# A hybrid SSD / attention block on one core: rotation, scan normalization and two scan sums on VectorE instead of GpSimd, key halves by DMA, and a different preparation of down blocks

## The chip, the core and the metric

The kernel is one launch on one core of a Trainium2 chip, in float32. What is timed is the device time of the launch in microseconds (us). TensorE (PE in the profile) multiplies matrices, VectorE (DVE), ScalarE (ACT) and GpSimd (POOL) do elementwise work, SyncE (SP) issues transfers; ACT and POOL issue transfers too, and each engine works through its own instructions in order.

## The reference

One block of a network for 512 tokens of width 2048. `u @ w_in` gives all projections at once; one half of the width goes through a state space scan (SSD), the other through attention with 16 query heads over 4 key heads in three branches (compressed, selected and window keys), of which the last two work on rotated queries and keys. Both halves meet in `w_out`; a gated feed-forward layer of width 5632 follows.

```python
def partial_rope(x, cos, sin):
    half = ROPE_DIM // 2                      # ROPE_DIM = 16 of 64
    c, s = cos[None, :, None, :], sin[None, :, None, :]
    x1, x2 = x[..., :half], x[..., half:ROPE_DIM]
    return jnp.concatenate([x1 * c - x2 * s, x2 * c + x1 * s, x[..., ROPE_DIM:]], axis=-1)
# ssd_mixer ends in
    return rmsnorm(y * jax.nn.silu(z), norm_w)
# nsa_mixer
    q_rot = partial_rope(q, cos, sin)
    ks, kw = partial_rope(ks, cos, sin), partial_rope(kw, cos, sin)
    k_cmp = compress_tokens(kc, cmp_w1_k, ...)   # silu(blocks @ w1) @ w2
    ...
    o = g[..., 0, :] * o_cmp + g[..., 1, :] * o_sel + g[..., 2, :] * o_win
# the block
    u = rmsnorm(h, attn_norm_w)
    z, xbc, dt_raw, q, kc, vc, ks, vs, kw, vw, gate_raw = split(u @ w_in)
    h = h + concatenate([y_ssd, y_att]) @ w_out
    v = rmsnorm(h, ffn_norm_w)
    h = h + (silu(v @ w_gate) * (v @ w_up)) @ w_down
    return rmsnorm(h, final_norm_w)
```

## The kernel before, in words

**Products in three passes.** A float32 product is made of three matmuls of a faster type (float32r): each operand is split into a high part and the rest. `a_hi` (L127) writes the high part with ScalarE, `lo` (L130) subtracts it and writes the low part, mostly with VectorE; `mul` (L136) and `add` (L139) are the other two helpers, called with the engine that is to do the work. Since all of them have one line each in the profile, groups are told apart by their tiles: `whi`/`wlo` are the two parts of a weight piece, `w1h`/`w1l` those of the compression's weight, `uq`, `rq` and `kh`/`kl` those of unrotated queries, rotated queries and rotated keys, `pth`/`ptl` those of transposed attention weights, `R` those of an item of the feed-forward layer.

**Up to 700 us: one stream of projection matmuls with other work let in.** `run_unit` (L235) runs one unit after the other: 128 columns of `w_in` or `w_out`, in pieces of four 128x128 blocks. `issue_split` splits a piece three pieces ahead (`LEAD`), and `sch.tick()` (`Sched`, L76) after each three matmuls lets generators go on: a `yield 6` means "go on after six more ticks", and `sch.wait` waits for a flag. The generators are the evacuations of finished units (`ev_z`, `ev_kc`, `ev_vs`, `ev_ks`, `ev_q`), the key compression (`compress`, L663) and `attention` (L851). PE's order follows from these ticks; in this part the order of the other engines is made by a scheduler, which runs a model of the engines.

- `ev_z` (L587) forms y·silu(z) for eight pieces t, sends it to DRAM (`gy_d`) and adds its squares into `acc2`, by GpSimd (L615 calls `add`, the profile has L139, tile `acc`). Behind the eighth, `ms_parts` (L638) loads each piece, multiplies it by the norm's row with GpSimd (tile `gy`), and splits it with the norm's weight as a scale.
- `compress` loads 16 pieces of w1 by transfers on GpSimd's queue (L676, `w1r`, four buffers), splits them and multiplies.
- `rope` (L775) sends the two swapped 8-row halves of each of two heads to a tile `sw` by four transfers on GpSimd's queue, while VectorE multiplies by cosines (`ro`); `rope2` (L786) multiplies `sw` by signed sines and adds, both by GpSimd. `q_stack` (L816) splits queries into two halves each: for `uq` GpSimd makes the low parts, for `rq` VectorE. `ev_ks` writes each rotated key half into both partition halves: eight splits, of which GpSimd makes two low parts.
- `attention` walks 112 items (4 groups, 4 heads, 7 blocks): `score` (matmuls, mask, exponential), `norm` (L920: reciprocal of the sum, times the gate, times the weights; it follows `score` in the same step), `trans` (transposes, three steps later: `LAG`), and `pvmm`. `compressed` (L858) does the compressed branch of a group.

**From 700 us: seven products instead of eight.** Gate, up and down use Strassen's scheme: of a block's four quarters 11, 12, 21, 22 seven combinations M1 to M7 are multiplied (Winograd's variant). Here every engine's order is written out. `steps` is the list of products and `items` that of their weights. `run_step` calls `prep(i + 2)` (L1235): `form` (L1219) makes an item's remaining sum on VectorE and its high part on ScalarE, `prep` its low part on VectorE; `form(i + 1)` is called ahead of the low part of i. `advance` (L1185) starts loads in list order whenever a buffer is free. The down projection takes 35 visits (`VISITS`): column block j, n rows of blocks. `quad` (L1392) gives a visit's combinations: S1 = 21 + 22 by GpSimd from loaded blocks (M5; M6 is 11 + S1), and S3 = 21 + 11 (M7), in visits 0 to 5 by GpSimd, later by a load on SP and a second, accumulating transfer on GpSimd's queue (L1208, L1210).

## Time and profile before

| | us |
|---|---|
| the three runs | 2185.95, 2178.3, 2175.37 (median 2178.3) |
| the profiled execution | 2179.35 |
| its span (first to last instruction) | 2177.5 |
| PE busy / DVE / ACT / POOL in the span | 2138.7 / 1778.4 / 1209.2 / 438.2 |
| granted TensorE clock, mean | 0.994 |

The profile is of one execution. A group row of it names line, engine, operation, the tiles it writes and reads with their shape, the count, then the busy time and the mean of one, then how long the engine sat idle just before such instructions and on whom it waited. A timeline row has the start, the length, the instruction, and in brackets the idle time before it with the engine that ended it. A window row has, for a stretch of time, the busy time of each engine with its number of instructions, the granted clock (1 is full), the share of the transfer engines and what they moved.

### The profile page before, as it was taken

How to read it: one execution, taken by the hardware profiler on the slowest of the kernel's cores; microseconds unless marked ns; L12 is line 12 of the kernel's file. 1: busy time of each engine (PE TensorE's matmuls, PEld its weight loads, DVE VectorE, ACT ScalarE, POOL GpSimd, SP SyncE). 2: the span in 40 equal slices, each digit the busy share in tenths (PEclk: the TensorE clock that was granted, in tenths of full speed). 3: DMA queues.
4: the chain of work that ended last, by engine and by line, in shares of the span. 5: the costliest groups of instructions: out<-in, count | busy, mean ns of one | idle time of the engine just before them, and what ended most of it. 6: DMA issues, size and time to landing. Idle time of an engine off the chain costs nothing.

```text
span 2177.5 us, 35329 instructions
## 1 busy us (share of the span) xinstructions
PE 2138.7 (98%) x12832; PEld 1890.0 (87%) x12832; DVE 1778.4 (82%) x2802; ACT 1209.2 (56%) x2023; POOL 438.2 (20%) x443
## 2 busy tenths in 40 slices
PE   9999999999999999999999999999999999999997
PEld 7888887888788888888888888888888899999897
DVE  6799767878886659888888888888888878887796
ACT  6555446686676657555555555555555443443353
POOL 0002234424431134100000000000000222222232
PEclk9999999999999999999999999999999999999999
DMA  6222342223464487888888788887888879888973
GB/s 214 92 69 73 129 139 88 76 98 110 142 214 116 110 256 211 242 220 252 219 255 239 216 260 213 253 239 218 254 220 264 312 192 326 240 275 211 315 197 100
DMA packets 179582, 428.22 MB, mean 197 GB/s; under 512 B 20784, under 2 KB 27952, under 8 KB 179408
## 3 DMA queue, kind: packets, MB, share of 16 engines
q1 hardware_dynamic: 140192, 322.74, 44.2%
q0 software_dynamic: 29552, 85.87, 20.2%
q10 hardware_dynamic: 9664, 17.36, 2.2%
q8 instruction: 101, 1.65, 0.3%
q14 instruction: 73, 0.60, 0.1%
HBM read 359.83 MB, written 62.39 MB: 194 GB/s over the span
## 4 chain that ended last, share of the span: by engine, by line
PE 84%; DVE 5%; DMA 4%; ACT 2%; issue 2%; POOL 1%; SPq 0%; DVEq 0%; ACTq 0%; POOLq 0%
PE ps_s L1269 21%; PE ps_g L1269 11%; PE ps_g L254 7%; PE ps_g L252 7%; PE ps_g L253 7%; PE ps_t L1269 6%; PE ps_g L1275 2%; PE ps_g L1273 2%; PE ps_g L1274 2%; PE ps_t L1275 2%; PE ps_t L1273 2%; PE ps_s L1275 2%; PE ps_t L1274 2%; PE ps_s L1273 2%; PE ps_s L1274 2%
## 5 line engine op out<-in xcount | busy, mean ns | idle before, releaser
L127 ACT ACTIVATE R<-Z 128x1024 fp32r<-128x1024 f32 (+4 forms) x444 | 405.9, 926 | 379.7 <-DVE Z L139 284.6
L130 DVE TENSOR_TENSOR R<-Z,R 128x1024 fp32r<-128x1024 f32 (+4 forms) x352 | 374.4, 1073 | 28.2 <-ACT R L127 9.8
L252 PE MATMUL ps_g<-u,whi 128*128 128x512 f32 x778 | 318.4, 409 | 2.1 <-ACT whi L127 2.1
L254 PE MATMUL ps_g<-u,wlo 128*128 128x512 f32 x778 | 307.2, 395 | 0.2
L253 PE MATMUL ps_g<-u,whi 128*128 128x512 f32 x778 | 306.1, 393 | 0.0
L1269 PE MATMUL ps_s<-u,R 128*128 128x512 f32 (+1 forms) x1160 | 251.3, 347 | 0.1
L1269 PEld LDWEIGHTS ps_s<-u,R 128*128 128x128 f32 x1160 | 188.7, 188 | 27.4 <-ACT A L1484 0.4
L130 DVE TENSOR_TENSOR wlo<-wraw,whi 128x512 fp32r<-128x512 f32 x203 | 154.6, 765 | 57.6 <-ACT whi L127 53.1
L127 ACT ACTIVATE whi<-wraw 128x512 fp32r<-128x512 f32 x203 | 125.9, 625 | 105.4 <-PE ps_g L253 85.6
L254 PEld LDWEIGHTS ps_g<-u,wlo 128*128 128x128 f32 x778 | 146.4, 188 | 33.1 <-DVE wlo L130 1.8
L252 PEld LDWEIGHTS ps_g<-u,whi 128*128 128x128 f32 x778 | 146.9, 189 | 24.9 <-ACT whi L127 2.4
L253 PEld LDWEIGHTS ps_g<-u,whi 128*128 128x128 f32 x778 | 147.4, 189 | 22.7
L1269 PE MATMUL ps_g<-u,R 128*128 128x512 f32 (+1 forms) x600 | 131.4, 347 | 0.0
L1269 PE MATMUL ps_t<-u,R 128*128 128x512 f32 x592 | 131.2, 348 | 0.0
L1269 PE MATMUL ps_g<-T,R 128*128 128x512 f32 (+1 forms) x584 | 125.6, 346 | 0.0
L1269 PE MATMUL ps_s<-V,R 128*128 128x512 f32 (+1 forms) x568 | 123.4, 348 | 0.0
L1269 PE MATMUL ps_s<-T,R 128*128 128x512 f32 (+1 forms) x552 | 122.9, 349 | 0.2 <-DVE R L130 0.2
L130 DVE TENSOR_TENSOR E<-Z,R 128x1024 fp32r<-128x1024 f32 (+1 forms) x92 | 110.8, 1204 | 7.5 <-ACT R L127 3.5
L139 DVE TENSOR_TENSOR Z<-Z 128x1024 f32<-128x1024 f32 (+4 forms) x99 | 107.8, 1088 | 5.0 <-POOL Z L139 3.2
L1269 PEld LDWEIGHTS ps_g<-u,R 128*128 128x128 f32 x600 | 98.0, 188 | 14.0
L1269 PEld LDWEIGHTS ps_t<-u,R 128*128 128x128 f32 x592 | 96.9, 188 | 14.0
L139 DVE TENSOR_TENSOR A<-ps_g,A 128x512 f32<-128x512 f32 (+1 forms) x102 | 67.3, 664 | 50.8 <-PE ps_g L1269 38.1
(520 smaller groups left out, 5561.8 us busy)
## 6 DMA issues: line engine op xcount, KB each, us to landing
Z<-in_w_up SPq DMA_DIRECT2D x95, 512.0 KB, 4.7
Z<-in_w_gate SPq DMA_DIRECT2D x95, 512.0 KB, 5.6
wraw<-in_w_in SPq DMA_DIRECT2D x156, 256.0 KB, 2.6
g_d<-A SPq DMA_DIRECT2D x147, 256.0 KB, 6.4
Z<-in_w_gate POOLq DMA_DIRECT2D x37, 512.0 KB, 7.7
Z<-in_w_up POOLq DMA_DIRECT2D x37, 512.0 KB, 7.9
u<-g_d SPq DMA_DIRECT2D x70, 256.0 KB, 5.4
Z<-in_w_down SPq DMA_DIRECT2D x55, 320.0 KB, 4.7
```

Of the source, the lines that this page charges most:

```text
L127: act.activation(dst, src, AF.Copy, scale=scale)
L130: eng.tensor_tensor(dst, src, f(hi), ALU.subtract)
L139: eng.tensor_tensor(o, a, b, ALU.add)
L252: pe.matmul(p, hi_t[i][:, j, :], ah, start=(k == 0), stop=False)
L253: pe.matmul(p, hi_t[i][:, j, :], al, start=False, stop=False)
L254: pe.matmul(p, lo_t[i][:, j, :], ah, start=False, stop=(k == u.nk - 1))
L1269: pe.matmul(o, w, x, start=start, stop=(k == n - 1 and o is q), skip_group_check=not fresh[0])
L1273: pe.matmul(q, h[:, k, :], ah, start=(k == 0), stop=False)
L1274: pe.matmul(q, h[:, k, :], al, start=False, stop=False)
L1275: pe.matmul(q, l[:, k, :], ah, start=False, stop=(k == s.blk.n - 1))
```

## The change

1. `ev_z`: the square sums of pieces 2 and 3 are added by VectorE.
2. `ms_parts`: VectorE multiplies by the norm's row and weight in one instruction, and the split takes no scale any more.
3. `rope`: VectorE multiplies by sines (`sw`) and by cosines (`ro`), and four accumulating transfers on GpSimd's queue add the swapped halves of `sw` into `ro`. `rope2` is gone, the sines' sign in the table is turned, and two cleared tiles aren't wanted any more.
4. `ev_ks`: each key half is split once, and a transfer copies both parts to the other partitions. `ev_q`: the low parts of `uq` are made by VectorE.
5. `norm`: it runs one step later; the reciprocals of two sides are one instruction; for the first side the product with the gate is made by ScalarE. `compressed` of group 0 has 10 ticks ahead of its transposes instead of 6.
6. Down: visits 22 to 27 form S3 by GpSimd from loaded blocks, as visits 0 to 5 do. In visit 0, the low part of an item is made before the sum of the next one (`late_sum`).

```diff
--- before.py
+++ after.py
@@ -23,6 +23,7 @@
 VISITS = [(0, 5), (1, 3), (2, 5), (3, 5), (4, 5), (5, 5), (6, 4), (7, 6), (1, 4), (6, 4), (3, 5), (4, 5), (2, 5), (5, 5),
           (0, 5), (7, 5), (1, 5), (6, 5), (2, 5), (7, 5), (5, 6), (0, 6), (3, 6), (4, 6), (1, 4), (6, 4), (2, 4),
           (0, 6), (2, 3), (6, 5), (7, 6), (5, 6), (3, 6), (4, 6), (1, 6)]
+BY_POOL = list(range(6)) + list(range(22, 28))
 GRING = 7
 WARM = 10
 NRAW0 = 2 * KD // 4
@@ -612,7 +613,7 @@
             else:
                 sq = sp.tile([128, 512], F32, tag="sq" if g == 0 else "yz", name="sq", bufs=1)
                 act.activation(sq, zs, AF.Square)
-                add(pool, acc2, acc2, sq)
+                add(dve if t in (2, 3) else pool, acc2, acc2, sq)
             sch.flags.add(("gy", t))
             if t == 7:
                 yield 12
@@ -623,15 +624,11 @@
 
     P2 = {}
 
-    def parts(dst, t, scale=None):
+    def parts(dst, t):
         h = wp.tile([128, 512], F32R, tag="whi", name="hp", bufs=4)
         l = wp.tile([128, 512], F32R, tag="wlo", name="lp", bufs=4)
-        if scale is None:
-            a_hi(h, t)
-            lo(dve, l, t, h)
-        else:
-            a_hi(h, t, scale=scale)
-            dve.scalar_tensor_tensor(l, t, scale, f(h), op0=ALU.mult, op1=ALU.subtract)
+        a_hi(h, t)
+        lo(dve, l, t, h)
         nc.gpsimd.dma_start(dst[0], f(h))
         nc.gpsimd.dma_start(dst[1], f(l))
 
@@ -641,9 +638,9 @@
             yield 8
             t = wp.tile([128, 512], F32, tag="raw", name="gy", bufs=4)
             nc.sync.dma_start(t, gy_d[k])
-            mul(pool, t, t, P2["row2"])
+            dve.scalar_tensor_tensor(t, t, col(C_SN + k), P2["row2"], op0=ALU.mult, op1=ALU.mult)
             yield 2
-            parts(gp_d[k], t, col(C_SN + k))
+            parts(gp_d[k], t)
             sch.flags.add(("gp", k))
 
     def ev_kc(g):
@@ -770,23 +767,16 @@
             sch.flags.add(("v", g))
         return ev
 
-    swt = []
-
     def rope(ap, qs):
 
-        R["nsw"] = R.get("nsw", 0) + 1
-        sw = swt[R["nsw"] % 2]
-        for b in (0, 64):
-            nc.gpsimd.dma_start(sw[b:b + 8, :], qs[b + 8:b + 16, :])
-            nc.gpsimd.dma_start(sw[b + 8:b + 16, :], qs[b:b + 8, :])
+        sw = ap.tile([128, 512], F32, tag="sw", name="sw", bufs=2)
+        mul(dve, sw, qs, ropes)
         ro = ap.tile([128, 512], F32, tag="ro", name="ro", bufs=1)
         mul(dve, ro, qs, ropec)
-        return sw, ro
-
-    def rope2(ap, sw, ro):
-        t = ap.tile([128, 512], F32, tag="fo", name="ro2", bufs=1)
-        mul(pool, t, sw, ropes)
-        add(pool, ro, ro, t)
+        for b in (0, 64):
+            nc.gpsimd.dma_start(ro[b:b + 8, :], sw[b + 8:b + 16, :], accum_op=ALU.add)
+            nc.gpsimd.dma_start(ro[b + 8:b + 16, :], sw[b:b + 8, :], accum_op=ALU.add)
+        return ro
 
     def ev_ks(g):
         def ev(p):
@@ -794,22 +784,17 @@
             ap = pools["att"][1]
             t = ap.tile([128, 512], F32, tag="qs", name="kt", bufs=2)
             mul(dve, t, p, rrow)
-            sw, ro = rope(ap, t)
+            ro = rope(ap, t)
             yield 4
-            rope2(ap, sw, ro)
             yield from after(("a", g - 2))
-            kh = ap.tile([128, 2, 512], F32R, tag="kh", name="kh", bufs=2)
-            kl = ap.tile([128, 2, 512], F32R, tag="kl", name="kl", bufs=2)
+            ks = ap.tile([128, 2, 2, 512], F32R, tag="ks", name="ks", bufs=2)
             for br in range(2):
-                s = ro[br * 64:br * 64 + 64, :]
                 own = slice(br * 64, br * 64 + 64)
-                for r in range(2):
-                    d = slice(r * 64, r * 64 + 64)
-                    a_hi(kh[d, br, :], s)
-                for r in range(2):
-                    d = slice(r * 64, r * 64 + 64)
-                    lo(dve if r == br else pool, kl[d, br, :], s, kh[own, br, :])
-            R["k", g] = (kh, kl)
+                d = slice(64 - br * 64, 128 - br * 64)
+                a_hi(ks[own, br, 0, :], ro[own, :])
+                lo(dve, ks[own, br, 1, :], ro[own, :], ks[own, br, 0, :])
+                nc.gpsimd.dma_start(f(ks[d, br]), f(ks[own, br]))
+            R["k", g] = (ks[:, :, 0], ks[:, :, 1])
             sch.flags.add(("k", g))
         return ev
 
@@ -827,8 +812,8 @@
             ap = pools["att"][1]
             t = ap.tile([128, 512], F32, tag="qs", name="qt", bufs=2)
             mul(dve, t, p, rrow)
-            sw, ro = rope(ap, t)
-            uq = q_stack(ap, "uq", 1, t, pool)
+            ro = rope(ap, t)
+            uq = q_stack(ap, "uq", 1, t, dve)
             yield 10
             yield from after(("sc", g - 2))
             if j == 0:
@@ -842,7 +827,6 @@
             dve.tensor_tensor(s2, pv[:, :, :, 0, :], cmask[:, :, None, :].to_broadcast([128, 4, 2, 32]), ALU.add)
             add(dve, s2, pv[:, :, :, 1, :], s2)
             yield 2
-            rope2(ap, sw, ro)
             yield from after(("h", g - 1 if j else g - 2, 1 if j else 3))
             R["rq", g, j] = q_stack(ap, "rq", 3, ro, dve)
             sch.flags.add(("q", g, j))
@@ -875,7 +859,7 @@
             mul(dve, sm[:, 2], sm[:, 2], gat[:, :, 12 * g:12 * g + 12:3])
             yield 2
             mul(dve, rows, rows, wide(2))
-            yield 6
+            yield 6 if g else 10
             if g:
                 yield from sch.wait(("pv", g - 1, 3, 0))
             p = ps_t()
@@ -919,14 +903,18 @@
 
         def norm(g, h, br, i):
             e, m = pr[g, h, br, i]
+            if not i:
+                m2 = m.rearrange("p (b c) -> p b c", b=2)
+                dve.reciprocal(m2[:, :, 2], m2[:, :, 1])
             for b, c, m in sides(br, i, m):
                 gc = (4 * g + h) * 3 + 1 + b
-                dve.reciprocal(m[:, 2:3], m[:, 1:2])
+                if i:
+                    dve.reciprocal(m[:, 2:3], m[:, 1:2])
                 if b:
                     dve.tensor_scalar(e[:, c], e[:, c], m[:, 2:3], gat[:, i, gc:gc + 1],
                                       op0=ALU.mult, op1=ALU.mult)
                 else:
-                    mul(dve, m[:, 3:4], m[:, 2:3], gat[:, i, gc:gc + 1])
+                    a_hi(m[:, 3:4], m[:, 2:3], scale=gat[:, i, gc:gc + 1])
                     a_hi(e[:, c], e[:, c], scale=m[:, 3:4])
 
         def trans(g, h, br, i):
@@ -996,8 +984,8 @@
             yield 1
             if 0 <= s - LAG < n:
                 trans(*items[s - LAG])
-            if s < n:
-                norm(*items[s])
+            if 0 <= s - 1 < n:
+                norm(*items[s - 1])
             yield PACE[s % len(PACE)]
             if 0 <= s - LAG - 1 < n and items[s - LAG - 1][2:] in ((2, 0), (1, 3)):
                 g, h, br, _ = items[s - LAG - 1]
@@ -1036,10 +1024,6 @@
         ap = open_pool("att")
 
         ap.tile([128, 2, 512], F32R, tag="uq", name="uq", bufs=1)
-        for i in range(2):
-            t = ap.tile([128, 512], F32, name=f"sw{i}")
-            pool.memset(t, 0.0)
-            swt.append(t)
         sch.flags.add("att")
 
     order = [U_DTG]
@@ -1237,14 +1221,20 @@
         form(upto)
         while nxt["item"] <= min(upto, len(items) - 1):
             i = nxt["item"]
-            form(i + 1)
+            early = i + 1 in late_sum
+            if not early:
+                form(i + 1)
             b = items[i][0]
             hl[i].append(hl_place(b))
             assert hl[i][1] is not None, (i, hz.busy)
             lo(dve, hl_ap(i, 1), b.ap(), hl_ap(i, 0))
             b.read()
             nxt["item"] += 1
+            if early:
+                form(i + 1)
             advance()
+
+    late_sum = []
 
     class Step:
         def __init__(self, blk, rhs, psum, after=None, before=None, sums=(), wide=False):
@@ -1878,10 +1868,10 @@
                 Step(blk, g_rhs(SEQ_END[n], a), one_bank, after=af(SEQ_END[n]), sums=sums)
 
     for v, (j, a, b) in enumerate(visits):
-        q = quad(w_down[j], a, b, by_dma=False, s3_by_pool=v < 6)
+        q = quad(w_down[j], a, b, by_dma=False, s3_by_pool=v in BY_POOL)
         for x in ("11", "12", "21", "22", "S1", "S3"):
             q[x].down = True
-        add_loads(q, "11 12 21 S3 22 S1" if v < 6 else "11 12 21 22 S1 S3")
+        add_loads(q, "11 12 21 S3 22 S1" if v in BY_POOL else "11 12 21 22 S1 S3")
         end = v - len(visits) + 2
         af, bk = d_end(j, end) if end >= 0 else d_after(j, a == 0, b == NP), banks(BANK_D)
         if end >= 0:
@@ -1894,6 +1884,8 @@
             continue
         for n, p in enumerate(SEQ_D):
             blk, sums = q["form"][p]
+            if v == 0 and sums:
+                late_sum.append(len(items))
             if n == 0 and v in (2, 3):
                 later[5 + (v == 3)] = len(items)
             s = Step(blk, g_rhs(p, a), bk(p), after=af(p),
@@ -2025,7 +2017,7 @@
     C = np.ones((64, S), np.float32)
     Sn = np.zeros((64, S), np.float32)
     C[0:8], C[8:16] = c, c
-    Sn[0:8], Sn[8:16] = -s, s
+    Sn[0:8], Sn[8:16] = s, -s
     k[:, K_RC:K_RC + 512] = np.concatenate([C, C])
     k[:, K_RS:K_RS + 512] = np.concatenate([Sn, Sn])
     return k
```

How the order of instructions moves at three places (names lack the row's number; one line is one instruction, or n of the same with xn).

GpSimd, before, where the square sums of the first four pieces end and the loads of the compression begin:

```order
L609 DMA gy_d<-zs 128x512
L139 TENSOR_TENSOR acc_95<-acc_95,sq 128x512
L676 DMA w1r<-in_w1k 128x512 x4
L676 DMA w1r<-in_w1v 128x512 x4
L609 DMA gy_d<-zs 128x512
L676 DMA w1r<-in_w1v 128x512
L139 TENSOR_TENSOR acc_95<-acc_95,sq 128x512
L676 DMA w1r<-in_w1v 128x512 x3
```

and now:

```order
L610 DMA gy_d<-zs 128x512
L673 DMA w1r<-in_w1k 128x512 x4
L673 DMA w1r<-in_w1v 128x512 x4
L610 DMA gy_d<-zs 128x512
L673 DMA w1r<-in_w1v 128x512 x4
```

Both sums `acc` are gone from this queue, the first of which stood ahead of the loads; VectorE has them.

VectorE, before, at the rotation of the first group's queries (`qt` is the evacuated projection, `ro` the rotated one):

```order
L136 TENSOR_TENSOR qt<-ps_g,rrow 128x512
L130 TENSOR_TENSOR kl<-ro,kh 64x512
L130 TENSOR_TENSOR wlo<-wraw,whi 128x512
L136 TENSOR_TENSOR ro<-qt,kc 128x512
L130 TENSOR_TENSOR wlo<-wraw,whi 128x512 x3
L136 TENSOR_TENSOR qt<-ps_g,rrow 128x512
L130 TENSOR_TENSOR wlo<-wraw,whi 128x512
L130 TENSOR_TENSOR rq<-ro,rq 64x512
L842 TENSOR_TENSOR sc<-ps_m,kc 128x4x64
L130 TENSOR_TENSOR rq<-ro,rq 64x512
```

and now:

```order
L137 TENSOR_TENSOR qt<-ps_g,rrow 128x512
L131 TENSOR_TENSOR wlo<-wraw,whi 128x512
L137 TENSOR_TENSOR sw<-qt,kc 128x512
L137 TENSOR_TENSOR ro<-qt,kc 128x512
L131 TENSOR_TENSOR uq<-qt,uq 64x512 x2
L131 TENSOR_TENSOR wlo<-wraw,whi 128x512 x2
L131 TENSOR_TENSOR rq<-ro,rq 64x512 x2
L827 TENSOR_TENSOR sc<-ps_m,kc 128x4x64
L131 TENSOR_TENSOR wlo<-wraw,whi 128x512
L140 TENSOR_TENSOR sc<-ps_m,sc 128x4x64
```

The product with the sines and the low parts of `uq` have come to this engine, and the low parts of `rq`, which wait for the four transfers into `ro`, stand two rows below (`wlo` between).

VectorE, before, in the first visit of the down projection (`Z` holds loaded blocks, `R` items; a row `Z<-Z` is an item's sum, `R<-Z,R` its low part):

```order
L136 TENSOR_TENSOR A<-A,rrow 128x1024
L139 TENSOR_TENSOR Z<-Z 128x640
L130 TENSOR_TENSOR R<-Z,R 128x640
L136 TENSOR_TENSOR A<-A,rrow 128x1024
L139 TENSOR_TENSOR A<-ps_g,A 128x256
L136 TENSOR_TENSOR A<-A 128x1024
L139 TENSOR_TENSOR Z<-Z 128x640
L130 TENSOR_TENSOR R<-Z,R 128x640 x2
```

and now:

```order
L137 TENSOR_TENSOR A<-A,rrow 128x1024
L131 TENSOR_TENSOR R<-Z,R 128x640
L140 TENSOR_TENSOR Z<-Z 128x640
L137 TENSOR_TENSOR A<-A,rrow 128x1024
L140 TENSOR_TENSOR A<-ps_g,A 128x256
L137 TENSOR_TENSOR A<-A 128x1024
L131 TENSOR_TENSOR R<-Z,R 128x640
L140 TENSOR_TENSOR Z<-Z 128x640
L131 TENSOR_TENSOR R<-Z,R 128x640
```

Each low part has moved ahead of the sum of the item that follows it.

## The prediction

> **What bounds the kernel now.** Read first: the page's busy times and its chain of waits.
>
> ```profile
> PE 2138.7 (98%) x12832; PEld 1890.0 (87%) x12832; DVE 1778.4 (82%) x2802; ACT 1209.2 (56%) x2023; POOL 438.2 (20%) x443
> PE 84%; DVE 5%; DMA 4%; ACT 2%; issue 2%; POOL 1%; SPq 0%; DVEq 0%; ACTq 0%; POOLq 0%
> ```
>
> TensorE is busy for 2138.7 of 2177.5 us, and the change leaves its matmuls alone. So what can be won is its idle time, 38.8 us, and the time it runs at a lower clock. The waits of TensorE over the whole span say where that lies:
>
> ```profile
> PE ps_t L1275 <- DVE R L130: 6.8, 7, 3.9
> PE ps_s L694 <- ACT w1h L127: 3.0, 1, 3.0
> PE ps_t L939 <- DVE ptl L130: 2.9, 3, 1.7
> PE ps_g L1273 <- ACT R L127: 2.4, 1, 2.4
> PE ps_g L252 <- ACT whi L127: 2.1, 1, 2.1
> PE ps_t L883 <- DVE sc L136: 1.4, 1, 1.4
> PE ps_v L959 <- DVE ptl L130: 1.0, 2, 0.6
> PE ps_s L906 <- DVE rq L130: 0.6, 1, 0.6
> ```
>
> (total us, number of waits, the longest.) Each is preceded by something late on VectorE, ScalarE or a queue. Four of them cost more than they last; windows behind them show the granted clock (the column after POOL):
>
> ```profile
> 282.00:300.00 18.00, 17.18 (x93) 15.06 (x94) 17.20 (x40) 13.70 (x32) 7.72 (x12) 0.91 0.63 195
> 549.00:600.00 51.00, 49.24 (x244) 40.07 (x244) 45.45 (x109) 33.96 (x80) 23.20 (x30) 0.97 0.50 158
> 1710.00:1720.00 10.00, 9.38 (x67) 9.38 (x68) 9.73 (x15) 6.57 (x13) 2.97 (x1) 0.83 0.62 196
> 2052.00:2062.00 10.00, 9.74 (x57) 9.45 (x58) 8.10 (x12) 2.84 (x6) 2.36 (x2) 0.68 1.02 357
> ```
>
> The missing clock is 18 x 0.09 = 1.6, 51 x 0.03 = 1.5, 10 x 0.17 = 1.7 and 10 x 0.32 = 3.2 us of work. The shortest stall with such a loss lasts 2.1 us, the longest without 1.74. The Trainium skill ("TensorE: Matmul & The Clock Gate", section "Why this matters for your kernels") asks to avoid idle gaps over about 3 us; by that the 2.1 and the 2.4 us stall would have cost no clock. The rows say otherwise, and I go by them; by the page, a stall that shrinks below 3 us at 1710 would give 1.7 us more than I count.
>
> **The change part by part.**
>
> *Square sums and the compression's loads.* GpSimd, then ScalarE, ahead of the first stall:
>
> ```profile
> 272.81 5.86 POOL L139 TENSOR_TENSOR acc<-acc,sq 128x512 f32<-128x512 f32 x1
> 278.62 2.19 POOL L676 DMA_DIRECT2D w1r<-in_w1k  x4
> 282.14 0.63 ACT L127 ACTIVATE w1h<-w1r 128x512 fp32r<-128x512 f32 x1 [5.38 <-DMA w1r<-in_w1k]
> ```
>
> A sum that took 5.86 us stands ahead of the loads. Without it they can be issued once the issue ahead of it ends, at 272.81, 5.8 us sooner, and land 5.8 us sooner; TensorE was late by 3.0 (the row of L694 above). So the stall and its clock go: 3.0 + 1.6 = **4.6 us**. VectorE gains two sums of 0.69 us (row `sc` below), beside matmuls.
>
> *Attention.* GpSimd's and VectorE's groups, 262 to 700 us and 300 to 700 us:
>
> ```profile
> L130 POOL TENSOR_TENSOR uq<-qt,uq 64x512 fp32r<-64x512 f32 x16 | 23.1, 1444 | 1.2
> L136 POOL TENSOR_TENSOR ro<-sw,kc 128x512 f32<-128x512 f32 x12 | 16.8, 1401 | 14.9 <-DMA sw<-kt 4.6 <-DVE em L911 3.8 <-DVE em L924 3.1
> L139 POOL TENSOR_TENSOR ro<-ro,ro 128x512 f32<-128x512 f32 x12 | 16.3, 1357 | 0.7
> L130 POOL TENSOR_TENSOR kl<-ro,kh 64x512 fp32r<-64x512 f32 x8 | 12.7, 1586 | 7.7 <-ACT kh L127 7.3
> L136 POOL TENSOR_TENSOR gy<-gy,row 128x512 f32<-128x512 f32 x8 | 10.5, 1316 | 32.4 <-DVE ptl L130 14.2 <-DMA gy<-gy_d 13.3 <-DVE sm L867 4.7
> ...
> L780 POOL DMA_DIRECT2D sw<-qt x16 | 8.3, 516 | 22.0 <-DVE qt L136 22.0
> ```
>
> ```profile
> L130 DVE TENSOR_TENSOR wlo<-wraw,whi 128x512 fp32r<-128x512 f32 x98 | 79.8, 817 | 19.7 <-ACT whi L127 17.6 <-PE ps_v L953 1.6
> ...
> L136 DVE TENSOR_TENSOR em<-em,gat 128x1 f32<-128x1 f32 x55 | 16.4, 298 | 1.2
> ...
> L136 DVE TENSOR_TENSOR sc<-sc,sm 128x512 f32<-128x512 f32 x4 | 2.7, 685 | 0.0
> ```
>
> GpSimd loses 23.1 + 16.8 + 16.3 + 12.7 + 10.5 = 79 us. VectorE takes over 12 products with sines, 16 low parts and 8 fuller products, 36 x 0.69 = 25 us, and gives up the 16.4 us of `em`. It also gets its own speed back: the same `wlo` would take 98 x (0.817 - 0.685) = 13 us less. Ops between tiles in SBUF are drawn out while GpSimd works; this 256-wide one took twice a 512-wide `sc`, and the stall of 1.74 came behind it:
>
> ```profile
> 447.94 1.38 POOL L139 TENSOR_TENSOR acc<-acc,sq 128x512 f32<-128x512 f32 x1 [1.58 <-ACT sq L614]
> 448.09 1.38 DVE L926 TENSOR_SCALAR e<-e,em,gat 128x256 f32<-128x256 f32 x1
> 450.94 0.44 PE L939 MATMUL ps_t<-ident,e 128*128 128x128 f32 x2 [1.74 <-DVE ptl L130]
> ```
>
> So VectorE ends at 25 - 16 - 13 = -4 us, at least not fuller. ScalarE gets some 55 one-column products and gives up 8 high parts. Its smallest op in the trace has one column, too:
>
> ```profile
> L913 ACT ACTIVATION_READ_ACCUMULATOR e<-e,em 128x1 f32 x108 | 20.3, 188 | 0.0
> ```
>
> 55 x 0.19 = 10 us, in 400 in which it idles a third (34 of 51 us busy in the window at 549); the product for the gate now follows on the engine that uses it. Free, unless ScalarE is held for long. The stalls here sum to 2.9 + 2.1 + 1.4 + 1.0 + 0.6 = 8.0, with the clock 9.5 us. The first two in time (the queries' at 341, the compressed branch's at 365, which gets four ticks, 12 matmuls of 0.2 us by the same window, more) go: 0.6 + 1.4 = 2.0. Of the other 7.5 I take half, 3.8, between bounds of 0 and 7.5: some have causes that stay (the `acc` above). **5.8 us**.
>
> What speaks against it is the new wait. Low parts of `rq` now stand in VectorE's queue behind two issues twice, that is four of 0.516 us, and a landing:
>
> ```profile
> DMA to landing us min/median/max: 1.7/2.7/5.9
> gp_d<-hp POOLq DMA_DIRECT2D x8, 256.0 KB, 2.6
> ```
>
> (The first row is that of the transfers into `sw`, which have the size and queue of the new ones.) That is 2.1 + 2.7 = 4.8 us, where GpSimd took 2.1 for issues and 2 x 1.44 + 1.40 + 1.36 = 5.6 for `uq` and `ro` before. In the first group four instructions (4 x 0.69 = 2.8 us) stand between on VectorE, so it waits about 2 us, and ScalarE, which makes the high parts first, as long. Weight pieces are queued behind both, but they are split three pieces, 3 x 12 x 0.2 = 7 us, ahead of TensorE. It fits; I price it at zero, between a gain of nothing and a loss of 2 us for each of 12 rotations. The key copies hold 256 KB each. Nothing in the trace moves that much between partitions; the nearest row, to DRAM, lands in 2.6 us (second row), and TensorE wants a group's keys many units later. Zero.
>
> *Visit 0.* VectorE's timeline ahead of the 3.9 us stall:
>
> ```profile
> 1702.67 0.83 DVE L139 TENSOR_TENSOR Z<-Z 128x640 f32<-128x640 f32 x1 [1.47 <-POOL Z L139]
> 1703.42 0.82 DVE L130 TENSOR_TENSOR R<-Z,R 128x640 fp32r<-128x640 f32 x1
> ...
> 1708.22 1.61 DVE L139 TENSOR_TENSOR Z<-Z 128x640 f32<-128x640 f32 x1
> 1709.76 1.77 DVE L130 TENSOR_TENSOR R<-Z,R 128x640 fp32r<-128x640 f32 x2
> ```
>
> The low part that TensorE waits for comes at 1709.76, behind a sum of 1.61. Ahead of it, it starts at 1708.22 and takes 0.82 to 1.61: TensorE goes on 0.75 to 1.5 us sooner. I take 1.1; a stall of 2.8 still costs the clock. **1.1 us**.
>
> *Visits 22 to 27.* The stall at 2052:
>
> ```profile
> 2038.17 2.57 POOL L139 TENSOR_TENSOR Z<-Z 128x768 f32<-128x768 f32 x1 [17.37 <-DVE A L139]
> 2042.21 0.87 POOL L1210 DMA_DIRECT2D A<-in_w_down  x1 [1.46 <-DVE Z L139]
> 2051.16 0.84 ACT L127 ACTIVATE R<-A 128x768 fp32r<-128x768 f32 x1 [5.82 <-DMA A<-in_w_down]
> ```
>
> The accumulating transfer of visit 27's S3 is issued behind GpSimd's sum, takes from 2042.2 to 2051.1, and TensorE waits 2.44 us and loses 3.2 of clock, 5.6 in all. With a sum by GpSimd (2.57 us at most) in its place S3 is there before 2046. Six visits with 30 row blocks in all lose two transfers of 64 KB for each block, 3.9 MB, 11 us at the 357 GB/s of the last window above. Against it: block 22 of visit 27 now comes behind 13 instead of 8 of TensorE's other operands in SP's queue, and six sums run beside VectorE. I subtract 0.8 us (0 to 5). **4.8 us**.
>
> The sum is 4.6 + 5.8 + 1.1 + 4.8 = 16.3 us; the profiled execution took 2179.35, so 2163 beside it. The median of the three runs lies 1 us lower, so the forecast is **2162 us**.
>
> **The rivals.** *The stalls of attention only move* (new waits for transfers in place of the old): nothing is won there, 10.5 are, 2168; between 2168 and 2173 if another term is half. For it: VectorE is as full as before (89% at 549), and waits in order for transfers. Against: the rotation's chain is 2.9 us shorter. *Visit 27 keeps its stall* at M6, which waits for block 22: the gain there is -0.8 instead of 4.8, so 2168. For it: five operands more ahead in SP's queue; against: 11 us less to move. *All goes*: 3.7 more from attention, 1 from small waits, 2157. *Slower*: the accumulating transfers are late at every rotation, and TensorE stops each time for 2.1 us with 1.5 of clock, as at 549. From six of the twelve rotations on (6 x 3.6 = 22) it eats the 10.5 us of the other terms and the 11 us of the bound below; at eight it is 29 - 10.5 = 18 us slower, 2196. For it: landings of up to 5.9 us. Against: issues of 0.5 us beside a VectorE that is 89% busy. The Trainium skill ("SBUF — State Buffer", section "SBUF: two separate sides") says that GpSimd can be locked out of writing a transfer's descriptors by some VectorE instructions, which would make this rival; by the issue times here it does not happen.
>
> **How the numbers follow.** Forecast 0.52; attention only moves 0.20; visit 27 keeps its stall 0.10; all goes 0.10; slower 0.08. A difference under 0.5%, 11 us, can't be told from none here. The forecast, "all goes" and half of the third (its price is near the bound) are faster than 2167: 0.67. Same is the rest of these, 0.20 + 0.05 = 0.25; slower 0.08. The range goes from 2152 (all goes, visit 0's clock too, and the 3 us by which the lowest run lies under the median) to 2176 (the first rival at its worst and those 3 us).
>
> **What would show it.** Right: `acc` of 5.9 us gone, `w1r` landed before 278, no wait at L694; GpSimd's attention groups gone and `wlo` near 0.69 us; waits `rq` <- DMA on VectorE of some 2 us without one of TensorE at L906; at visit 0 a stall of 2.3 to 3.1; none at visit 27's M7. Wrong: stalls on `whi` or `wlo` after a DVE or ACT wait for `ro` or `ks`, a lower clock between 300 and 700, a wait of M6 in visit 27 over 2 us.

## The result, and the profile after

The changed kernel takes 2164.85 us (median of six runs, 2161.98 to 2166.61); the kernel before 2178.14 us (six runs, 2172.62 to 2185.95). The ratio is 0.994, with an interval of 0.9923 to 0.9957, that is 9 to 17 us won. The forecast was 2162 us, in a range of 2152 to 2176. The profiled execution is the fastest of the six, 2161.98 us with a span of 2160.1, against 2179.35 and 2177.5 before.

The busy times and the chain of waits of the changed kernel:

```profile
PE 2130.1 (99%) x12832; PEld 1885.6 (87%) x12832; DVE 1763.3 (82%) x2760; ACT 1217.0 (56%) x2079; POOL 375.5 (17%) x391
PE 91%; DVE 5%; DMA 2%; issue 1%; ACT 0%; SPq 0%; DVEq 0%; POOL 0%; ACTq 0%
```

TensorE issues as many matmuls as before, and its part of the chain went from 84 to 91%. Waits of TensorE over the whole span (total, number, longest):

```profile
PE ps_t L1265 <- DVE R L131: 4.5, 5, 3.3
PE ps_g L1265 <- DVE R L131: 3.0, 5, 1.3
PE ps_s L1265 <- DVE R L131: 1.9, 5, 0.6
PE ps_v L947 <- DVE ptl L131: 1.7, 1, 1.7
...
PE ps_t L1263 <- ACT R L128: 1.1, 1, 1.1
...
PE ps_m L760 <- DVE vt L137: 1.0, 1, 1.0
...
PE ps_t L927 <- DVE ptl L131: 0.6, 1, 0.6
```

Gone are the waits on `w1h` (3.0), on `whi` (2.1), on `sc` (1.4), on `rq` (0.6), and the 2.4 on ScalarE's `R`. Of attention's 8.0 us, 2.3 are left (L947, L927). New are 1.0 on `vt` and 1.1 on ScalarE's `R` (L1263). In the feed-forward part the waits on VectorE's `R` did not become fewer: 4.5 + 3.0 + 1.9 us, where there were 6.8 + 1.4 + 0.3. Windows of it, the first two at the times of two windows of before, the third for attention as a whole, the fourth around visit 0's stall:

```profile
282.00:300.00 18.00, 18.00 (x117) 16.22 (x116) 17.27 (x42) 12.13 (x28) 4.36 (x8) 1.00 0.56 180
549.00:600.00 51.00, 50.45 (x267) 42.43 (x265) 44.87 (x121) 38.53 (x97) 12.08 (x18) 1.00 0.71 229
300.00:700.00 400.00, 396.80 (x2061) 333.33 (x2060) 301.14 (x787) 279.63 (x678) 82.44 (x109) 1.00 0.43 128
1686.00:1700.00 14.00, 9.53 (x60) 9.00 (x59) 10.20 (x14) 5.63 (x12) 4.17 (x3) 0.76 0.98 344
```

The clock (the column behind GpSimd's) was 0.91 and 0.97 in the first two, and is 1.00. In the third GpSimd works 82.44 of 400 us, most of it in issuing transfers; VectorE is busy for 12.9 us less than in the same window of before (301.14 against 314.01). In the fourth the clock is 0.76, so visit 0's stall still costs some clock, as the prediction counted.

**Where the time went, by stages.** All kernels of this study issue 12,832 matmuls. So the time from the start of one matmul to the start of another, counted by its number in the program, can be set against the same stretch in the trace of the kernel before. The table gives these differences in us, for seven stretches named by their times in that trace (negative is sooner). Most rows are one profiled execution each, and one execution can differ from the next by up to 3.7 us in a stretch, as the second trace of the kernel before shows in its own row.

| kernel | 169–300 | 300–702 | 702–1686 | 1686–1729 | 1729–1984 | 1984–2078 | 2078–2166 |
|---|---|---|---|---|---|---|---|
| the changed kernel | −4.7 | −9.7 | −0.1 | +1.3 | −0.6 | −3.3 | −0.1 |
| before, second trace (`c_before`) | −0.2 | −1.3 | +3.0 | +1.2 | −0.6 | −3.7 | +0.9 |
| `e1_sums` | −4.7 | −0.6 | −0.2 | +0.3 | −1.0 | −3.1 | +0.9 |
| `e4_att` | −0.5 | −11.2 | +0.4 | +1.3 | −1.2 | −1.8 | +0.5 |
| `e2_nolate` | −4.7 | −8.9 | +0.4 | +1.0 | −0.6 | −2.6 | −0.1 |
| `e3_s3dma` | −4.7 | −8.6 | 0.0 | +1.4 | −0.7 | −3.2 | 0.0 |
| `a5_normonly` | −0.4 | −1.4 | +0.3 | +0.5 | −1.5 | −1.1 | +0.3 |
| `a2_norm` | −4.7 | −10.7 | +1.0 | +2.0 | −1.4 | −1.9 | 0.0 |
| `a7_rope` | −4.7 | −8.2 | +0.5 | +1.6 | +0.1 | −2.8 | +0.5 |
| `a8_uqgy` | −4.7 | −7.1 | +0.2 | +1.6 | −1.8 | −3.3 | −0.1 |
| `a3_pool` | −4.7 | −6.5 | 0.0 | +1.2 | −1.1 | −3.3 | +0.6 |
| `a6_wide` | −4.7 | +3.7 | −0.1 | +1.4 | −1.1 | −1.3 | +0.6 |
| `b1_less` | −4.7 | −10.6 | +0.5 | −0.4 | −1.3 | −3.3 | +0.6 |

The first two columns hold the gain of this trace, 14.4 of 17.3 us. What the experiments below had to settle: whether the columns 1686–1729 and 1984–2078 are the work of the change at all, and what in attention is worth 9.7 us where 5.8 were expected.

### The profile page after: what moved, and what is told of

Read it like the earlier page. It is cut to its first block, busy times and chain, and to the rows that moved or that the text cites. A ratio compares the mean times of both kernels' runs of the same rounds, so it can differ in the third digit from the quotient of the medians.

```text
span 2160.1 us, 35230 instructions
## 1 busy us (share of the span) xinstructions
PE 2130.1 (99%) x12832; PEld 1885.6 (87%) x12832; DVE 1763.3 (82%) x2760; ACT 1217.0 (56%) x2079; POOL 375.5 (17%) x391
## 4 chain that ended last, share of the span: by engine, by line
PE 91%; DVE 5%; DMA 2%; issue 1%; ACT 0%; SPq 0%; DVEq 0%; POOL 0%; ACTq 0%
PE ps_s L1259 21%; PE ps_g L1259 11%; PE ps_g L253 8%; PE ps_g L255 8%; PE ps_g L254 8%; PE ps_t L1259 6%; PE ps_g L1265 2%; PE ps_g L1263 2%; PE ps_g L1264 2%; PE ps_t L1265 2%; PE ps_s L1265 2%; PE ps_s L1263 2%; PE ps_t L1263 2%; PE ps_s L1264 2%; PE ps_t L1264 2%; PE ps_v L947 2%
## 5 line engine op out<-in xcount | busy, mean ns | idle before, releaser
L131 DVE TENSOR_TENSOR wlo<-wraw,whi 128x512 fp32r<-128x512 f32 x203 | 142.9, 707 | 60.1 <-ACT whi L128 57.1
L128 ACT ACTIVATE R<-A 128x1024 fp32r<-128x1024 f32 (+3 forms) x72 | 67.8, 942 | 75.0 <-DVE A L140 51.7
```

The lines of the kernel that those rows point to most:

```text
L128: act.activation(dst, src, AF.Copy, scale=scale)
L131: eng.tensor_tensor(dst, src, f(hi), ALU.subtract)
```

## The experiments

The theory is the prediction's: four gains in four places, the largest by taking GpSimd's long instructions away from beside VectorE. Against it stand, place by place: that a term is nothing but one execution's bad moment (visit 0, visits 22 to 27), and that attention's gain is that of shorter chains or of the new `norm`, not of VectorE's speed.

### The square sums alone, and attention alone

`e1_sums` is the kernel before with one line of the change:

```diff
-                add(pool, acc2, acc2, sq)
+                add(dve if t in (2, 3) else pool, acc2, acc2, sq)
```

> The kernel before with the first part alone: the square sums of pieces 2 and 3 by VectorE. Theory (GpSimd's queue order): the loads w1r are issued some 6 us sooner, the wait of 3.0 us at L694 and the lower clock behind it go, nothing else moves: 4.6 to 4.8 us faster than before, 0.21%. Rival (the loads were late for another reason, or the next piece is late instead): at least half of the 3.0 us stays, as a wait of the same line, and the gain is under 2 us.

Measured: 2172.92 us against 2178.65, ratio 0.9975 (0.9965 to 0.9985), that is 3.3 to 7.6 us won. `e4_att` is the changed kernel with the attention parts (2 to 5 of the list) alone:

```diff
-BY_POOL = list(range(6)) + list(range(22, 28))
+BY_POOL = list(range(6))
...
-                add(dve if t in (2, 3) else pool, acc2, acc2, sq)
+                add(pool, acc2, acc2, sq)
...
-            if v == 0 and sums:
-                late_sum.append(len(items))
```

> The kernel before with the attention parts alone (rotation, keys, uq, gy, norm, ten ticks); sums of ev_z and the down projection as before. Theory: the attention part is worth what the traces show between 300 and 700 us, 9.6 us, by itself, and the waits at L694, visit 0 and visit 27 stay as before: 9.6 us faster, 0.44%. Rival: half of it hung on GpSimd's queue being free earlier after the first part, or on where the clock dips fall: 5.8 us or less.

Measured: 2165.80 us, ratio 0.9936 (0.9918 to 0.9955), that is 10 to 18 us won: as much as by the whole change, within the intervals. The times thus show that most of the gain comes with attention, but not what each of the other parts adds; that can be read from the stages only. In the changed kernel the loads stand where the prediction put them. GpSimd's and ScalarE's timeline:

```profile
272.21 0.55 POOL L610 DMA_DIRECT2D gy_d<-zs  x1 [8.12 <-DVE zs L137]
273.30 0.68 POOL L673 DMA_DIRECT2D w1r<-in_w1k  x1 [0.54 <-DVE w1l L131]
277.88 0.63 ACT L128 ACTIVATE w1h<-w1r 128x512 fp32r<-128x512 f32 x1 [1.12 <-DMA w1r<-in_w1k]
```

ScalarE has the first piece at 277.88 (282.14 before), and the stall with its low clock is gone in all ten kernels that have this line: −4.7 in the first column, against −0.2 to −0.5 in the three other new traces. But a wait comes a few us later, in the changed kernel and, with 0.96 at 312.40, in `e1_sums`:

```profile
313.22 0.66 PE L760 MATMUL ps_m<-ident,vt 128*128 128x128 f32 x4 [0.97 <-DVE vt L137]
```

TensorE transposes `vt` right behind the compression's last matmuls. `e4_att`, without the two moved sums, has no such wait. So the sums are worth 4.7 − 0.3 − 1.0 = 3.4 us in the traces. What is left is attention's: 300–702 is −11.2 with attention alone, and −0.6 with the sums alone.

### Visit 0: the low part ahead of the sum

`e2_nolate` is the changed kernel without the order of visit 0:

```diff
-            if v == 0 and sums:
-                late_sum.append(len(items))
```

> The changed kernel without late_sum: in visit 0 the sum of the next item is made ahead of the low part again. Theory (from the traces): late_sum makes the sum of M3 later, so its block comes free later, its load is issued 1.2 us later, and the wait of 1.29 us some 14 us behind the first is its price; without late_sum the first wait grows from 3.3 to about 3.9 us, that later one falls to 0.2: 0.7 to 1.2 us faster than the changed kernel. Rival (the prediction): late_sum wins 1.1 us, so this is 1.1 us slower, and the later wait stays, since it comes from the lower clock or the load itself.

Measured: 2163.17 us, ratio 0.9926 (0.9908 to 0.9944), which the changed kernel's 0.994 does not beat. TensorE's stalls of over 1 us at this place, in the changed kernel:

```profile
1691.93 0.39 PE L1263 MATMUL ps_t<-V,R 128*128 128x256 f32 x1 [1.14 <-ACT R L128]
1695.76 0.58 PE L1265 MATMUL ps_t<-V,R 128*128 128x256 f32 x1 [3.33 <-DVE R L131]
1710.11 0.39 PE L1265 MATMUL ps_g<-V,R 128*128 128x256 f32 x1 [1.29 <-DVE R L131]
```

and in `b1_less` (below), which has the old order, where it is the only one:

```profile
1694.95 0.58 PE L1261 MATMUL ps_t<-V,R 128*128 128x256 f32 x1 [3.89 <-DVE R L131]
```

The big stall did shrink, as predicted: it lasts 3.33, 2.40, 3.02, 2.22, 2.27, 2.28 and 2.22 us in the seven traces with the new order, 3.75 to 3.93 in the seven without. What was gained comes back. VectorE's rows in the changed kernel show the low part moved ahead, and the next one waiting:

```profile
1694.10 1.61 DVE L131 TENSOR_TENSOR R<-Z,R 128x640 fp32r<-128x640 f32 x1
1695.63 0.81 DVE L140 TENSOR_TENSOR Z<-Z 128x640 f32<-128x640 f32 x1
1697.30 0.83 DVE L131 TENSOR_TENSOR R<-Z,R 128x640 fp32r<-128x640 f32 x1 [0.86 <-ACT R L128]
```

The sum is now late, so is ScalarE's high part of it, and VectorE waits 0.86 us for that; from then on TensorE waits twice for later items: 1.19 to 1.21 us some 10 us behind the stall in six of the seven, and 1.04 to 1.29 us some 15 us behind it in all seven (of the traces with the old order four have a wait of over 0.5 us there, of 0.66 to 1.04). Over the whole stretch 1686–1729 the seven with the new order stand at +1.2 to +2.0 (mean 1.5), the seven with the old one at −0.4 to +1.3 (mean 0.6). By these means it costs 0.9 us where 1.1 was expected to be won, but the two groups differ in other parts as well. The pair that differs in this alone, the changed kernel and `e2_nolate`, lies 0.3 us apart, and in `e2_nolate` the later wait does not fall to 0.2 us, as was expected, but lasts 1.04. So no gain shows here; that something is lost is likely, and not shown. That the later sum makes a block free later, and so a load, is argued from the order and wasn't tried apart.

### Visits 22 to 27, and a second trace of the kernel before

`e3_s3dma` is the changed kernel with S3 by transfer from visit 6 on:

```diff
-BY_POOL = list(range(6)) + list(range(22, 28))
+BY_POOL = list(range(6))
```

> The changed kernel with S3 of visits 22 to 27 by an accumulating transfer again. Theory (traces): the wait of 2.4 us in visit 27 and its 3.2 us of lower clock come back, and 2.2 us of small waits for VectorE in visits 23 to 27 go: 3.5 us slower than the changed kernel. Rival (the prediction): the small waits are worth 0.8 only, 4.8 slower. Third: the wait in visit 27 was an accident of one execution, and it is at most 1 us slower.

Measured: 2164.30 us, ratio 0.9936 (0.992 to 0.9952): the same as with the change. `c_before` is the kernel before once more, with nothing changed:

> The kernel before once more, unchanged, for a second trace. Theory (the 2.4 us wait in visit 27 with its lower clock is that of one execution, as the kernels with the same down projection that showed 1.0 to 1.4 us suggest): under 1.5 us here, no lower clock behind it. Rival (it belongs to the moment at which this program gets there): 2.2 to 2.7 us again, with the lower clock; the waits at 282, 341 to 600 and 1710 are within 0.3 us of the first trace in both cases.

One run, 2177.8 us. The stall of 2.44 us on which this term of the prediction was built lasts 0.72 us here,

```profile
2051.63 0.39 PE L1273 MATMUL ps_g<-T,R 128*128 128x256 f32 x1 [0.72 <-ACT R L127]
```

and 1.03 in `e3_s3dma`, which forms S3 in the same way:

```profile
2037.54 0.38 PE L1263 MATMUL ps_g<-T,R 128*128 128x256 f32 x1 [1.03 <-ACT R L128]
```

It lasts 0.7 to 2.4 us in the seven traces that form S3 by transfer (the other four: 1.19, 1.40, 1.08, 2.27). In the stretch 1984–2078 these stand at 0 for the first trace of before and −1.1 to −3.7 for the six others (mean of all seven −2.3); the seven that form it by GpSimd at −1.3 to −3.3 (mean −2.6). The transfer's wait is gone with the change, but small waits on VectorE have come in its place (1.3 + 1.2 + 1.1 us in this stretch of the changed kernel). The change is worth 0.3 us here, less than one execution differs from the next. The 3.3 us by which the changed kernel's trace beats the first trace of before come from a bad moment of that first execution.

### Attention: the new `norm`

`a5_normonly` is the kernel before with part 5 of the change, except the ticks of `compressed`; `a2_norm` is the changed kernel without it (the ticks stay):

```diff
-            if 0 <= s - 1 < n:
-                norm(*items[s - 1])
+            if s < n:
+                norm(*items[s])
```

and within `norm`, one reciprocal for each side and VectorE's product with the gate.

> The kernel before with the new norm alone (one step later, merged reciprocals, the gate's product by ScalarE); GpSimd keeps all its work. Theory (GpSimd beside VectorE costs the larger part): 2 to 4 us faster than before, and the waits at 341, 365 and 549 us stay. Rival (the order of norm is what mattered): 7 us or more faster.

> The changed kernel with norm as before: in the step of its score, two reciprocals, the gate's product by VectorE. Theory (VectorE's load and order decide): VectorE gets 55 products of 0.16 us back, 9 us, and waits for sums of exponentials that were just started; waits of TensorE for ptl grow by 2 to 4 us, 2 to 4 us slower than the changed kernel. Rival (GpSimd's removal alone brought the gain): within 1 us of the changed kernel.

Measured: `a5_normonly` 2175.35 against 2175.04, ratio 0.9999 (0.9987 to 1.0012); `a2_norm` 2163.00, ratio 0.9951 (0.9933 to 0.9969), which is within the changed kernel's. The new `norm` brings nothing that shows, alone (2 to 4 us were expected) or with the rest (a loss of 2 to 4 us without it was expected); in the stretch 300–702 the two traces of an otherwise changed kernel without it stand at −10.6 and −10.7, the three with it at −8.6 to −9.7. The group of `em` shows why there was little to move. In the changed kernel on ScalarE:

```profile
L128 ACT ACTIVATE em<-em,gat 128x1 f32<-128x1 f32 x56 | 16.1, 287 | 6.9 <-DVE em L912 6.4 <-DVE em L908 0.4
```

and in `a2_norm` on VectorE:

```profile
L137 DVE TENSOR_TENSOR em<-em,gat 128x1 f32<-128x1 f32 x56 | 8.8, 156 | 1.2
```

It took 298 ns on VectorE in the kernel before, with GpSimd's work beside it. Without that work it takes 156 ns, less than ScalarE's 287. The ten ticks of `compressed` were not undone alone: they are in all kernels with the attention parts, and the wait for `sc` that is gone (1.4 us) may be theirs.

### Attention: GpSimd beside VectorE

Two theories were left: the gain comes from the chains (rotation, `uq`, key halves) being shorter, or from VectorE's instructions not being drawn out by GpSimd any more. `a3_pool` and `a6_wide` are the changed kernel with GpSimd kept busy by sums that nobody uses, at the places where it worked before (behind each rotation's transfers, behind `uq`, behind `gy`). In `a3_pool` they are short, three of 160 columns each time one stands in `a6_wide`:

```diff
+        R["dm"] = ap.tile([128, 160], F32, name="dm")
...
+    def idle_work(n):
+        for _ in range(3 * n):
+            add(pool, R["dm"], R["dm"], R["dm"])
```

> The changed kernel with idle work put on GpSimd in attention: 144 sums of a scratch tile of 128x160 that nobody reads, 36 us or more in 320 to 640 us, behind the issues of each rotation, each uq and each piece gy. No other engine's work or dependence is changed. Theory (contention): VectorE's operations between SBUF tiles are drawn out beside GpSimd's, the mean of wlo between 300 and 700 us goes from 0.70 back to 0.75 or more, TensorE's waits there come back in part, 3 us or more slower than the changed kernel. Rival (what was won is the shorter chain, GpSimd no longer in the way of rq and of keys): wlo stays, within 1 us of the changed kernel.

Measured: 2165.65 us, ratio 0.996 (0.9945 to 0.9975). In `a6_wide` they have 512 columns, as the removed ones had (`kc` in its rows is the constants, of which the sines are a part), and `sw` has one buffer to make room (no wait of VectorE for it shows). They also read two tiles, where the short ones read one tile twice; what that alone does was not tried:

```diff
+        R["dm"] = ap.tile([128, 512], F32, name="dm")
...
+    def idle_work(n):
+        for _ in range(n):
+            add(pool, R["dm"], R["dm"], ropes)
```

> As the kernel with idle work, but with long sums: 48 of 512 columns from two tiles (scratch and the table of sines), some 1.4 us each as the rotation's were, 65 us or more, at the same places; VectorE's tile of products with sines has one buffer for it instead of two. The short sums (81 us of 0.5 us each) cost 3.2 of the 9.7 us and drew wlo out from 0.70 to 0.73 only. Theory (contention, by long operations): wlo at 0.78 or more, 6 us or more lost between 300 and 700 us against the changed kernel. Rival (chain): again 3 us or less, however long the operations are.

Measured: 2177.27 us against 2177.26, ratio 1.0002 (0.9989 to 1.0016). The whole gain is gone: what the square sums win in the first column is eaten with it. GpSimd's and VectorE's groups from 300 to 700 us, in `a6_wide`:

```profile
L140 POOL TENSOR_TENSOR dm<-dm,kc 128x512 f32<-128x512 f32 x48 | 77.4, 1612 | 2.9
```

```profile
L131 DVE TENSOR_TENSOR wlo<-wraw,whi 128x512 fp32r<-128x512 f32 x96 | 80.8, 845 | 20.4 <-ACT whi L128 17.8 <-ACT pth L128 1.9 <-ACT e L128 0.2
```

in `a3_pool`:

```profile
L140 POOL TENSOR_TENSOR dm<-dm 128x160 f32<-128x160 f32 x143 | 89.3, 625 | 9.9
```

```profile
L131 DVE TENSOR_TENSOR wlo<-wraw,whi 128x512 fp32r<-128x512 f32 x99 | 71.7, 726 | 22.4 <-ACT whi L128 19.4 <-ACT pth L128 1.5 <-DMA gp_d<-lp 0.7
```

and in the changed kernel:

```profile
L131 DVE TENSOR_TENSOR wlo<-wraw,whi 128x512 fp32r<-128x512 f32 x100 | 69.8, 699 | 24.3 <-ACT whi L128 21.6 <-ACT pth L128 1.9 <-ACT e L128 0.2
```

The 77.4 us of idle work are about the 79 that the change took away. `wlo` has 845 ns again (817 before). With more time of GpSimd, 89.3 us, in short pieces, it has 726, less than the 750 that the theory had asked for, and 300–702 stands at −6.5, ten us better. Of these ten, 3.3 are lower clock behind two stalls of `a6_wide` (0.80 over the 8 us from 361.09, 0.79 from 417.75). So it isn't only how long GpSimd works, but how long one of its instructions holds up what is due on VectorE. TensorE's longest waits in `a6_wide`, 300 to 700 us, are not for `rq`, `ks` or a transfer, as longer chains would have it:

```profile
PE ps_v L954 <- DVE ptl L131: 3.3, 2, 1.9
PE ps_t L934 <- ACT e L128: 2.6, 1, 2.6
PE ps_s L897 <- DVE em L902: 1.5, 2, 1.0
```

How VectorE is held up, its timeline in `a6_wide` shows, beside two stretches in which GpSimd works without a break:

```profile
331.84 9.77 POOL L140 TENSOR_TENSOR dm<-dm,kc 128x512 f32<-128x512 f32 x5
...
345.38 12.35 POOL L140 TENSOR_TENSOR dm<-dm,kc 128x512 f32<-128x512 f32 x7
```

```profile
340.37 1.78 DVE L137 TENSOR_TENSOR sw<-qt,kc 128x512 f32<-128x512 f32 x1
...
348.40 1.67 DVE L131 TENSOR_TENSOR rq<-ro,rq 64x512 fp32r<-64x512 f32 x1
...
350.17 0.41 DVE L834 TENSOR_TENSOR sc<-ps_m,kc 128x256 f32<-128x256 f32 x1
...
351.07 0.70 DVE L131 TENSOR_TENSOR rq<-ro,rq 64x512 fp32r<-64x512 f32 x1
...
352.82 0.69 DVE L131 TENSOR_TENSOR wlo<-wraw,whi 128x512 fp32r<-128x512 f32 x1
353.43 1.26 DVE L858 TENSOR_SCALAR sm<-sm 128x16 f32<-128x16 f32 x1
...
354.94 1.63 DVE L860 TENSOR_TENSOR sc<-sc,sm 128x512 f32<-128x512 f32 x1
```

`sw`, the first `rq` and the last `sc`, which read two tiles in SBUF, take about as long as one GpSimd sum (12.35 / 7 = 1.76 us), where alone they take 0.69; the one with an operand from the accumulators (`ps_m`) takes its usual 0.41 in the same stretch. Not every such instruction is hit: the second `rq` and `wlo` read two tiles as well and take 0.70 and 0.69. And `sm`, which reads one tile, takes 1.26, against 0.16 in the changed kernel. The Trainium skill ("SBUF — State Buffer", section "Who interferes with whom") states this rule: a VectorE instruction with two inputs in SBUF and a GpSimd instruction that reads SBUF contend, and the second one blocks until the first ends. The three long rows agree with that, and so does the mean of `wlo`, 726 ns beside short sums and 845 beside long ones. Why the second `rq` and `wlo` are spared, these rows do not show, and the rule as put here does not cover `sm`.

Two parts of the change were undone alone. `a7_rope` has the rotation as before (transfers into `sw`, product and sum by GpSimd), `a8_uqgy` has the low parts of `uq` and the products for `gy` by GpSimd as before:

```diff
-            ro = rope(ap, t)
+            sw, ro = rope(ap, t)
...
+            rope2(ap, sw, ro)
```

> The changed kernel with the rotation as before: swapped halves by transfer, product with sines and sum by GpSimd (33 us of 1.4 us each). Theory (contention): a share of GpSimd's 79 us, 33/79 of the loss of all, 4 us lost between 300 and 700. Rival (the chain to rq): 7 us or more, with waits for rq or ks. Third (nothing hangs on this part): under 1.5 us.

```diff
-            uq = q_stack(ap, "uq", 1, t, dve)
+            uq = q_stack(ap, "uq", 1, t, pool)
...
-            dve.scalar_tensor_tensor(t, t, col(C_SN + k), P2["row2"], op0=ALU.mult, op1=ALU.mult)
+            mul(pool, t, t, P2["row2"])
```

> The changed kernel with the low parts of uq and the norm row's product of gy by GpSimd, as before (23 and 10 us, 1.3 to 1.45 us each). VectorE has 24 operations less. Theory (contention): 3 to 5 us lost between 300 and 700. Rival (VectorE's load bounds): 1 us gained or more, the wait of 1.7 us at 536 for ptl goes. Third: the two cancel, within 1 us.

Measured against 2177.26: 2165.28 us, ratio 0.995 (0.9931 to 0.9968), and 2167.82 us, 0.996 (0.9945 to 0.9975). In the stretch 300–702 they stand at −8.2 and −7.1, where the three traces with the whole change have a mean of −9.1: each costs 1 to 2 us alone, by one trace, where the theory had 4 and 3 to 5. `wlo` has 730 and 750 ns. In `a8_uqgy` TensorE also waits once for `uq` by GpSimd itself, 1.2 us, so there the longer chain is a part of the loss. The parts of the gain don't add up: each time 33 of GpSimd's 79 us came back for a little, while 77 us of long sums at the same places cost everything that the change had won. How much of the remaining 6 us is the key halves, how much the ten ticks, and how much comes only when GpSimd is as busy as in `a6_wide`, stays open: `kl` was not undone alone, and the bursts of `a6_wide` are denser than GpSimd's work was in the kernel before.

### The parts that were worth something

`b1_less` is `a2_norm` without the parts on the down projection: the square sums, rotation, `uq`, `gy`, key halves and the ten ticks are left.

```diff
-BY_POOL = list(range(6)) + list(range(22, 28))
+BY_POOL = list(range(6))
...
-            if v == 0 and sums:
-                late_sum.append(len(items))
```

> The first part and the attention parts without the new norm; down projection as before (no late_sum, S3 of visits 22 to 27 by transfer). Theory (the down parts and the norm are worth nothing each): 12 to 15 us faster than before, 0 to 2 us faster than the changed kernel. Rival (the prediction's terms for the down projection hold): 5 us slower than the changed kernel, 8 faster than before.

Measured: 2163.71 us against 2177.26, ratio 0.9944 (0.9922 to 0.9966): with half of its parts it is as fast as the whole change. That it is faster than that, the intervals don't show.

## Why the prediction was right, and where it wasn't

The time came within 3 us of the forecast, but of the four terms only the first came near its size, and attention came at the upper end of its bounds. From the stage table:

| term | forecast | measured | from |
|---|---|---|---|
| square sums, loads | 4.6 | 3.4 | 169–300, less the wait on `vt` |
| attention | 5.8 (2.0 to 9.5) | 9.4 | 300–702, below |
| visit 0 | 1.1 (0.75 to 1.5) | −0.9 | 1686–1729, means of seven (−0.3 by `e2_nolate`) |
| visits 22 to 27 | 4.8 | 0.3 | 1984–2078, means of seven |
| sum | 16.3 | 12.2 | runs: 13.3 (9 to 17) |

Attention: with the `vt` wait taken out, the four traces that have all its parts stand at −10.7, −9.9, −9.6 and −11.2 (mean −10.3), and the three traces of attention as before at 0, −1.3 and −1.6 (mean −1.0); the difference is 9.4.

**Square sums.** Mechanism and place right: no `acc` ahead of the loads, `w1r` there before 278, no stall at L694, clock 1.00. The term failed by what stood behind it: the step counted two sums on VectorE "beside matmuls" as free, and didn't ask which wait ends last next. It was `vt` on that engine, 1.0 us.

**Attention.** The mechanism named is the one shown: GpSimd draws out VectorE's instructions. `wlo` came to 699 ns where 685 was expected, the 256-wide product of 715 ns to 404. What failed is the size: "of the other 7.5 I take half". In the changed kernel all went but 2.3 us of idle time, 5.2 of the 7.5. The sum `acc` that was to stay is still there (1.29 us at 435.82), but the 256-wide product starts behind it, at 437.56, and takes 0.41. In `e2_nolate` and `e3_s3dma` a stall that is left at 537 to 538 still loses clock. And the listed idle time understates a stall. Three rows of TensorE in the changed kernel:

```profile
314.17 0.40 PE L255 MATMUL ps_g<-u,wlo 128*128 128x512 f32 x1
314.41 0.40 PE L253 MATMUL ps_g<-u,whi 128*128 128x512 f32 x1
314.64 0.39 PE L254 MATMUL ps_g<-u,whi 128*128 128x512 f32 x1
```

They start 0.23 us apart but are listed with 0.40, since each ends behind the start of the next; so the idle time before the next instruction counts some 0.17 us too little at each wait, 1.4 for the eight waits of before. 5.7 us of idle time that went (8.0 − 2.3), 1.5 of clock and 0.17 x 6 for the waits that went make 8.2 of the 9.4. The rest is within what one execution differs from the next.

The step on the new wait held. ScalarE waits for the accumulating transfers, and their landing, in the changed kernel:

```profile
ACT ks L128 <- DMA ro<-sw: 5.7, 6, 2.0
...
ACT rq L128 <- DMA ro<-sw: 4.0, 3, 1.4
```

```profile
DMA to landing us min/median/max: 2.3/3.1/7.4
```

Waits of 2 us at most, for twelve rotations, and none of TensorE on `rq`: the weight pieces ahead covered it, as predicted, and the rival "slower" had nothing. The term for `norm`, a part of the 5.8 without a price of its own, was wrong in sign or nothing: it rested on 298 ns a product, which the same change brings down to 156, and took ScalarE's price from an accumulator read of 188 ns where the product takes 287.

**Visit 0.** The stall shrank to about the predicted 2.3 to 3.1 us (2.22 to 3.33 in seven traces). The step that failed is that this is a gain: "TensorE goes on 0.75 to 1.5 us sooner" took the end of the stall as the end of the matter. The sum that was moved behind is itself due, and later waits came in exchange.

**Visits 22 to 27.** The step that failed is to price a stall of one execution as if every run had it: 2.4 + 3.2 of clock there, 0.72 without any loss of clock in the next trace of the same kernel. Which part of that stall comes in every execution wasn't asked. The rival "visit 27 keeps its stall" named another cause for nearly the same time.

So the total came near by luck: 6.5 us too much in the last two terms and 1.2 in the first met 3.6 too little in attention. The interval of 9 to 17 us can't tell 12.2 from 16.3; only the stages show that the terms were off. The prediction's bound for what can be told from none, 11 us, was too wide: the 5.7 us of `e1_sums` stand clear of none.

## What to carry to other kernels

Where VectorE is near full and its instructions read two tiles in SBUF, take long GpSimd instructions out from beside it before anything finer, or try them in shorter pieces: an instruction that runs into one can take as long as it does. A stall seen in one trace is priced only when a second trace of the same kernel has it. An instruction moved ahead of another makes the other late, so ask who waits for that one before counting the gain.
